# Splitting each load of weights into its high and low part in one step or in two

## The chip, the cores and the metric

The kernel runs on one core of a Trainium2 chip. The core has a matrix engine (TensorE, PE in the profile; its weight loads stand as PEld), a vector engine (DVE), a scalar engine (ACT), GpSimd (POOL) and a queue processor (SP) that issues most of the DMAs. Every engine works through its own instructions in the order in which the program lists them, and waits on semaphores for the others. The metric is the device time of one execution in microseconds. Before the change it was 1292.62 us, the median of three runs (1292.37 to 1294.42).

## The reference

One layer of an encoder over 1024 tokens of width 1024, in float32:

```
h = rmsnorm(x, norm1_w);  z = h @ w_in                      # 1024 x 2852
A: 8 heads of sparse attention: an indexer scores keys, the 256 best per query are kept,
   softmax over those with a position bias, times values
B: 8 heads of chunkwise retention with rotary, group norm and a swish gate
x = x + concat(A, B) @ w_out                                # 1024 x 1024
h2 = rmsnorm(x, norm2_w)
x = x + (silu(h2 @ w_gate) * (h2 @ w_up)) @ w_down          # hidden width 2816
```

All of the large products go through weights that are used once: w_in, w_out, w_gate, w_up and w_down.

## The kernel before

To keep float32 accuracy at the speed of the shorter format, each factor is split into a high part, which is the value rounded, and a low part, which is the rest. A product is then three matmuls: high by high, high by low and low by high. For the weights this is done on the chip, chunk by chunk. A chunk is what one pass of TensorE over 512 tokens needs: 256 columns by 1024 rows for the projections and for gate and up, or 512 columns by 512 rows for the down projection. The first chunk of each half of the input projection is 292 columns wide.

The function `pieces` (lines 277 to 311) prepares a chunk. Its generator `fill` goes over the chunk's loads. A load is a DMA of 1024 columns into a tile `wraw`, of which there are three in rotation (line 292); a chunk of 256 or 512 columns has two loads, the last chunks of the down projection one, a chunk of 292 columns four loads of 584 columns. The load is cut into `SUB` = 2 parts. For each part ACT copies and rounds it into `whi` (line 306; the very first load of the program goes through DVE instead, line 304), and DVE subtracts that from `wraw` into `wlo`. The subtraction of a part is held back in `late` until the next part, or the next load, has its turn. The tiles `whi` and `wlo` exist twice, so while TensorE works on one chunk the next one can be prepared.

The order of all instructions is fixed when the program is built. The code walks through the matmuls of the projections; after every three of them `tick` (line 937) asks the threads in `THREADS` (weights "w", selection "sel", attention "att", and so on) whether their next step may be placed there. A step runs a generator up to its next `yield`. It may be placed when the time at which the thread's last step ends, by the planner's own estimates, lies 0.7 us back, and when the estimated work that waits on DVE and on ACT is at most 4.0 us. The estimates are made in `charge` (line 865): an ACT copy of n columns is put at 0.06 + n/1200 us, a DVE subtraction at 0.07 + n/960 us. When a chunk is needed, `weights` (line 982) places whatever is left of its steps at once, and opens the next chunk. So the parts of the weights stand in the queues of ACT and DVE between the small steps of selection, attention and retention.

The second half of the feed-forward block takes gate and up through another path, `chunk_parts` (line 356), in which a load of 1024 columns is split in one step already; it does not go through `pieces`. The down projection there does.

Of the kernel before, what the change touches and what calls it, by code (L numbers as in the profile page):

```python
# [25 lines left out]
C_Q, C_C, C_QB, C_KB, C_VB, C_GB = 0, 512, 804, 1316, 1828, 2340  # L26
NEG = -1.0e30
BIG = 3.0e38
SUB = 2
WARM = 11  # L30
VALUES, PAIRS, GATES = 4, 4, 2

# [86 lines left out]
class Layer:  # L119
# [157 lines left out]
    def pieces(self, loads, step, n, rows):  # L277

        nc = self.nc
        first, self.warm = not self.warm, True  # L280
        hi, lo = self.wpair()
        hi = hi[:, :rows * n].rearrange("p (k n) -> p k n", n=n)
        lo = lo[:, :rows * n].rearrange("p (k n) -> p k n", n=n)

        def fill():
            late = None
            for i, parts in enumerate(loads):
                if late:
                    late()
                    late = None  # L290
                tag, bufs = ("sc", 2) if first and i == 3 else ("wraw", 3)
                raw = (self.at_ if tag == "sc" else self.sb)([128, 1024], tag=tag, bufs=bufs)[:, :step * n].rearrange("p (k n) -> p k n", n=n)
                o = 0
                for src, w in parts:
                    nc.sync.dma_start(raw[:, :, o:o + w], src.rearrange("(k p) n -> p k n", p=128))
                    o += w
                ks = slice(i * step, i * step + step)
                sub = step // SUB if step % SUB == 0 else step
                for k0 in range(0, step, sub):
                    ks = slice(i * step + k0, i * step + k0 + sub)  # L300
                    if late:
                        late()
                    if first and i == 0:
                        nc.vector.tensor_copy(hi[:, ks, :], raw[:, k0:k0 + sub, :])
                    else:
                        nc.scalar.activation(hi[:, ks, :], raw[:, k0:k0 + sub, :], AF.Copy)
                    late = lambda ks=ks, raw=raw, k0=k0: nc.vector.tensor_tensor(
                        lo[:, ks, :], raw[:, k0:k0 + sub, :], hi[:, ks, :].bitcast(F32), op=OP.subtract)
                    yield
            late()  # L310
        return (hi, lo), fill()

    def order(self, j0, g):
# [1087 lines left out]
```

## Time and profile before

| | |
|---|---|
| median of three runs | 1292.62 us |
| the profiled execution | 1296.16 us |
| span of its instructions | 1294.4 us |
| PE busy | 1259.0 us, 97% |
| DVE busy | 999.0 us, 77% |
| ACT busy | 788.7 us, 61% |
| POOL busy | 57.3 us, 4% |

The profiled execution is 3.5 us above the median, and 1.8 us of it lie outside the span. A busy time is the time in which at least one of the engine's instructions is on record; the records of neighbouring instructions overlap, so a busy share near 1 is not an engine at its peak. All instructions stand under one line of the code, L99, because a helper issues them; the tiles' names tell them apart. `d` is the PSUM tile of the projections, `t` and `l` are those of attention and retention.

### The profile page before, as it was taken

The numbers are of one execution on the slowest core, as the hardware profiler recorded it, in microseconds if no ns is written. First come the engines' busy times: TensorE is split into PE (matmuls) and PEld (weight loads), VectorE is DVE, ScalarE is ACT, GpSimd is POOL, SyncE is SP. The second block draws the span as 40 slices with busy tenths as digits, with TensorE's granted clock in tenths as the row PEclk, the third lists the DMA queues.
The fourth block names the chain that finished last, engine by engine and source line by source line (L and its number), as shares of the span: only waits on it lengthen the run. The fifth ranks groups of instructions, "written<-read, shape, count | busy, mean of one in ns | idle before, by whom it ended". The sixth has DMA issues, their size and how long they took to land.

```text
span 1294.4 us, 22648 instructions
## 1 busy us (share of the span) xinstructions
PE 1259.0 (97%) x8363; PEld 1133.8 (88%) x8363; DVE 999.0 (77%) x2592; ACT 788.7 (61%) x1764; POOL 57.3 (4%) x68
## 2 busy tenths in 40 slices
PE   8799998999999999999999999999999999999998
PEld 7799898999999888888888878888988999898987
DVE  6679899888978887878787695645488787776866
ACT  7778977655695778468658944433375454453533
POOL 1401011010120000000000000000000000000000
PEclk8899999999999999999999999999999999999999
DMA  8433213221232132322223222225434242433311
GB/s 270 159 83 85 73 45 105 76 64 52 66 122 91 53 95 68 96 66 73 90 66 96 67 82 81 66 75 203 130 98 147 66 131 72 124 87 110 98 49 66
DMA packets 157791, 121.33 MB, mean 94 GB/s; under 512 B 8176, under 2 KB 137840, under 8 KB 157552
## 3 DMA queue, kind: packets, MB, share of 16 engines
q1 hardware_dynamic: 151744, 111.14, 28.7%
q10 hardware_dynamic: 5936, 8.74, 2.0%
q8 instruction: 65, 1.06, 0.3%
q14 instruction: 46, 0.38, 0.1%
HBM read 115.67 MB, written 4.19 MB: 93 GB/s over the span
## 4 chain that ended last, share of the span: by engine, by line
PE 75%; DVE 11%; ACT 7%; issue 3%; DMA 2%; POOL 1%; SPq 0%; ACTq 0%; POOLq 0%; DVEq 0%
PE d L99 64%; PE t L99 9%; DVE wlo L99 3%; ACT junk L99 3%; PE l L99 2%; DVE L L99 1%; ACT whi L99 1%; ACT Thi L99 1%; ACT waste L99 1%; DMA bias<-in_near_dram 1%; DVE plo L99 1%; DMA wraw<-in_w_down_dram 0%; POOL rc L99 0%; DVE Tlo L99 0%; DVE junk L99 0%
## 5 line engine op out<-in xcount | busy, mean ns | idle before, releaser
L99 PE MATMUL d<-whi,Thi 128*128 128x256 f32 (+2 forms) x1136 | 352.0, 310 | 6.2 <-ACT Thi L99 4.3
L99 PE MATMUL d<-wlo,Thi 128*128 128x256 f32 (+2 forms) x1136 | 342.1, 301 | 1.6 <-DVE wlo L99 1.5
L99 PE MATMUL d<-whi,Tlo 128*128 128x256 f32 (+2 forms) x1136 | 341.7, 302 | 0.0
L99 PEld LDWEIGHTS d<-whi,Thi 128*128 128x128 f32 x1136 | 216.2, 190 | 20.0 <-ACT Thi L99 6.7
L99 PEld LDWEIGHTS d<-wlo,Thi 128*128 128x128 f32 x1136 | 216.4, 191 | 10.1 <-DVE wlo L99 2.3
L99 PEld LDWEIGHTS d<-whi,Tlo 128*128 128x128 f32 x1136 | 216.8, 191 | 8.7 <-DVE Tlo L99 1.1
L99 ACT ACTIVATE whi<-wraw 128x512 fp32r<-128x512 f32 (+1 forms) x300 | 171.7, 616 | 69.0 <-PE d L99 52.6
L99 DVE TENSOR_TENSOR wlo<-wraw,whi 128x512 fp32r<-128x512 f32 (+1 forms) x302 | 197.2, 674 | 6.6 <-ACT whi L99 5.8
L99 ACT ACTIVATE junk<-sc,tc 128x384 bf16<-128x384 f32 (+5 forms) x186 | 163.6, 879 | 33.8 <-DVE tc L99 30.1
L99 PE MATMUL d<-Phi,whi 128*128 128x256 f32 x616 | 172.4, 280 | 1.7 <-ACT u L99 1.0
L99 PE MATMUL d<-Phi,wlo 128*128 128x256 f32 x616 | 171.9, 280 | 1.6 <-DVE wlo L99 1.6
L99 PE MATMUL d<-Plo,whi 128*128 128x256 f32 x616 | 171.6, 279 | 0.0
L99 PE MATMUL d<-Thi,whi 128*128 128x512 f32 (+1 forms) x368 | 143.1, 389 | 0.0
L99 PE MATMUL d<-Tlo,whi 128*128 128x512 f32 (+1 forms) x368 | 141.2, 384 | 0.2 <-DVE Tlo L99 0.2
L99 PE MATMUL d<-Thi,wlo 128*128 128x512 f32 (+1 forms) x368 | 141.2, 384 | 0.0
L99 PEld LDWEIGHTS d<-Phi,whi 128*128 128x128 f32 x616 | 116.6, 189 | 3.1 <-ACT u L99 1.8
L99 PEld LDWEIGHTS d<-Phi,wlo 128*128 128x128 f32 x616 | 116.3, 189 | 2.0 <-DVE wlo L99 1.9
L99 PEld LDWEIGHTS d<-Plo,whi 128*128 128x128 f32 x616 | 116.3, 189 | 0.4
L99 DVE TENSOR_TENSOR x<-d,x 128x512 f32<-128x512 f32 (+1 forms) x64 | 39.1, 623 | 64.2 <-PE d L99 56.5
L99 ACT ACTIVATE whi<-S 128x1024 fp32r<-128x1024 f32 x44 | 45.4, 1056 | 69.4 <-PE d L99 57.0
L99 PEld LDWEIGHTS d<-Thi,wlo 128*128 128x128 f32 x368 | 69.1, 188 | 14.9
L99 PEld LDWEIGHTS d<-Tlo,whi 128*128 128x128 f32 x368 | 69.2, 188 | 12.1 <-DVE Tlo L99 0.5
(334 smaller groups left out, 2349.7 us busy)
## 6 DMA issues: line engine op xcount, KB each, us to landing
wraw<-in_w_down_dram SPq DMA_DIRECT2D x44, 512.0 KB, 3.7
wraw<-in_w_in_dram SPq DMA_DIRECT2D x24, 512.0 KB, 3.8
wraw<-in_w_gate_dram SPq DMA_DIRECT2D x44, 256.0 KB, 3.1
wraw<-in_w_up_dram SPq DMA_DIRECT2D x44, 256.0 KB, 3.5
quad<-in_w_gate_dram SPq DMA_DIRECT2D x44, 256.0 KB, 3.6
quad<-in_w_up_dram SPq DMA_DIRECT2D x44, 256.0 KB, 4.3
wraw<-in_w_in_dram SPq DMA_DIRECT2D x32, 256.0 KB, 3.4
wraw<-in_w_out_dram SPq DMA_DIRECT2D x16, 512.0 KB, 3.8
```

The costliest lines, as they stand in the source:

```text
L99: return f(*args, **kw)
```

## The change

`SUB` becomes 1, so that each load is split by one ACT copy and one DVE subtraction over all of its columns. The first chunk of the program keeps its two parts.

```diff
@@ -26,7 +26,7 @@
-SUB = 2
+SUB = 1
@@ -295,7 +295,7 @@
                 ks = slice(i * step, i * step + step)
-                sub = step // SUB if step % SUB == 0 else step
+                sub = step // (2 if first else SUB)
                 for k0 in range(0, step, sub):
                     ks = slice(i * step + k0, i * step + k0 + sub)
```

A chunk of two loads then has three steps in place of five, one of one load two in place of three, and the 292 column chunk of the second half five in place of nine.

## Rows read from the trace of the kernel before

**Rows 1.** The page: busy time, share and instructions of the engines
```profile
PE 1259.0 (97%) x8363; PEld 1133.8 (88%) x8363; DVE 999.0 (77%) x2592; ACT 788.7 (61%) x1764; POOL 57.3 (4%) x68
```

**Rows 2.** Waits of PE alone: us in total, times, longest us
```profile
PE t L99 <- ACT ct L99: 4.6, 2, 4.3
...
PE d L99 <- DVE wlo L99: 3.1, 3, 1.6
...
PE d L99 <- ACT whi L99: 1.7, 3, 1.1
...
PE d L99 <- DVE Tlo L99: 0.2, 1, 0.2
```

**Rows 3.** Busy time by stage: PE, PEld, DVE, ACT, POOL, clock, DMA share, GB/s
```profile
20.00:425.00 405.00, 389.33 (x3161) 374.20 (x3160) 339.88 (x1257) 289.38 (x828) 51.75 (x55) 0.99 0.31 90
425.00:884.00 459.00, 455.21 (x2314) 378.63 (x2313) 343.31 (x901) 298.99 (x598) 2.59 (x4) 1.00 0.25 76
```

**Rows 4.** Waits of all engines, the longest of ACT, columns as in rows 2
```profile
ACT whi L99 <- PE d L99: 156.0, 53, 9.2
```

**Rows 5.** Groups by form: shapes, count, busy us, mean ns, idle before, releasers
```profile
L99 DVE TENSOR_TENSOR wlo<-wraw,whi 128x512 fp32r<-128x512 f32 x288 | 191.3, 685 | 6.6 <-ACT whi L99 5.8
...
L99 ACT ACTIVATE whi<-wraw 128x512 fp32r<-128x512 f32 x288 | 166.9, 624 | 65.8 <-PE d L99 50.3 <-issue 6.9 <-DVE maA L99 5.2
...
L99 DVE TENSOR_TENSOR wlo<-S,whi 128x1024 fp32r<-128x1024 f32 x44 | 52.9, 1222 | 4.9 <-ACT whi L99 4.8
...
L99 ACT ACTIVATE whi<-S 128x1024 fp32r<-128x1024 f32 x44 | 45.4, 1056 | 69.4 <-PE d L99 57.0 <-DVE S L99 9.2 <-DVE cc L99 3.1
```

**Rows 6.** Timeline of ACT near 980 us: start, us, instruction, count
```profile
978.35 1.06 ACT L99 ACTIVATE whi<-S 128x1024 fp32r<-128x1024 f32 x1 [0.51 <-DVE S L99]
979.31 0.61 ACT L99 ACTIVATE th<-cc 128x512 f32<-128x512 f32 x1
...
984.40 2.18 ACT L99 ACTIVATE whi<-wraw 128x512 fp32r<-128x512 f32 x4
```

**Rows 7.** Timeline of DVE near 980 us
```profile
979.44 1.23 DVE L99 TENSOR_TENSOR wlo<-S,whi 128x1024 fp32r<-128x1024 f32 x1
980.59 0.69 DVE L99 SCALAR_TENSOR_TENSOR th<-th,cc 128x512 f32<-128x512 f32 x1
...
986.40 2.49 DVE L99 TENSOR_TENSOR wlo<-wraw,whi 128x512 fp32r<-128x512 f32 x4
```

**Rows 8.** Timeline of PE: the 292 column chunk of the second half
```profile
199.03 0.40 PE L99 MATMUL d<-whi,Thi 128*128 128x292 f32 x1 [1.06 <-ACT whi L99]
200.04 0.40 PE L99 MATMUL d<-whi,Thi 128*128 128x292 f32 x1 [0.61 <-DVE zqk L99]
```

**Rows 9.** Chain that ended last, in that stretch: start, us, what
```profile
195.44 2.83 DMA mb__3057<-in_xt_dram
...
199.57 0.42 DVE zqk L99
```

**Rows 10.** Groups by form, the waits of 256 column matmuls for low parts
```profile
L99 PE MATMUL d<-wlo,Thi 128*128 128x256 f32 x896 | 251.6, 281 | 0.3 <-DVE wlo L99 0.3
```

**Rows 11.** Timeline of ACT: second chunk, the bias load's issue, the last chunk
```profile
24.12 1.67 ACT L99 ACTIVATE whi<-wraw 128x512 fp32r<-128x512 f32 x3
...
38.09 0.34 ACTq L99 DMA_DIRECT2D bias<-in_near_dram  x1
...
1278.06 0.63 ACT L99 ACTIVATE whi<-wraw 128x512 fp32r<-128x512 f32 x1 [1.09 <-issue]
1278.65 0.63 ACT L99 ACTIVATE Thi<-th 128x512 fp32r<-128x512 f32 x1
```

**Rows 12.** Timeline of DVE: second chunk, the bias
```profile
24.78 1.90 DVE L99 TENSOR_TENSOR wlo<-wraw,whi 128x512 fp32r<-128x512 f32 x3
...
45.54 1.23 DVE L99 TENSOR_TENSOR bias<-bias,far 128x1024 f32<-128x1024 f32 x1 [3.95 <-DMA bias<-in_near_dram]
```

**Rows 13.** Timeline of PE: the second chunk's first matmul
```profile
26.53 0.28 PE L99 MATMUL d<-whi,Thi 128*128 128x256 f32 x1
```

## The prediction

> **What bounds the kernel now.** I read the page first: TensorE is on record as busy for 1259.0 of the 1294.4 us, DVE for 999.0 and ACT for 788.7 [rows 1]. So at most 35.4 us of the span are idle time of the engine that everything feeds, and a change that only shortens work on DVE and ACT can win no more than a part of that. The second view is the list of what TensorE waited for. It has 21 lines, which begin with 4.6 us for a small tile of the key path and end with 0.2 us [rows 2]; all together they are 38 waits and 30.7 us. The parts of the weights, the only thing this change makes, end six of them: 3.1 us for low parts and 1.7 us for high parts [rows 2]. The third view, the busy time by stage, says where there is anything to win or lose. From 20 to 425 us, in the input projection with attention beside it, TensorE idles 405.00 - 389.33 = 15.7 us, and DVE is busy for 84% of the stage; from 425 to 884 us, in the first half of the feed-forward block, it idles 459.00 - 455.21 = 3.8 us [rows 3]. Last, the waits of all engines show who leads: ACT stood before a copy into `whi` for 156.0 us in 53 waits until TensorE had let go of the buffer [rows 4]. The splitting thus works against the buffers, nearly a whole chunk ahead of its use, and not against the clock.
>
> **The change part by part.** The first part is the work itself. By the durations, two copies of 512 columns take 2 x 624 = 1248 ns on ACT and one of 1024 takes 1056; two subtractions on DVE take 2 x 685 = 1370 ns and one 1222 [rows 5]. There are 144 such loads (288 halves), so the durations promise 144 x 0.192 = 27.6 us less on ACT and 144 x 0.148 = 21.3 us less on DVE. That is too much, since neighbouring records overlap. Four copies of 512 in a row took 2.18 us, so each after the first adds (2.18 - 0.62) / 3 = 0.52 us, while the instruction behind a copy of 1024 starts 979.31 - 978.35 = 0.96 us after it [rows 6]. The saving is 2 x 0.52 - 0.96 = 0.08 us a load. On DVE it is 2 x (2.49 - 0.69) / 3 - (980.59 - 979.44) = 1.20 - 1.15 = 0.05 us [rows 7]. I take these: some 11.5 us of ACT and 7 us of DVE in the whole kernel, 1.5% and 0.7% of their busy time. All of it lies beside TensorE's work. Its worth on the path is 0; if that cover were gone the DVE share of it, 7 us, would show. The DMAs are as many and as large as before and stand in the same order on SP. Only the release of a `wraw` tile moves: from its copy's start it took 0.62 + 2 x 0.60 + 0.69 - 0.60, about 1.9 us, with two halves behind each other, and takes 1.06 + 1.22, about 2.3 us, with one. With three tiles in rotation, and splitting a chunk ahead, 0.4 us of delay to a prefetch is hidden: 0, and 0.4 us for each load where it isn't.
>
> The second part is what TensorE waits for directly. Of the six waits for parts, the 256 column chunks have 0.3 us [rows 10], and the 292 column chunk of the second half has 1.06 us at 199.03 us [rows 8]. The rest belongs to the first chunk and to the path of `chunk_parts`, which don't change. The wait at 199.03 looks like a gain: with five steps in place of nine that chunk would be done before its matmuls begin. But one block of matmuls later TensorE waits again, until 200.04, for a tile that DVE frees (`zqk`) [rows 8], and the chain of that stretch goes from a load of x, 195.44 to 198.27 us, to that DVE instruction and not through the weights [rows 9]. What is saved at 199.03 is therefore waited at 200.04. I put the direct waits at -0.2 us, with ends at -1.4 (both waits gone) and +0.4.
>
> The third part is the lead of the second chunk, the one place where a first part becomes urgent. Its copies start at 24.12 and its matmuls at 26.53 us [rows 11, 13], and its subtractions at 24.78 [rows 12]. With one step the first high part is ready at 24.12 + 1.06 = 25.2, and the low part at about 25.2 + 1.22 = 26.4 us, just in time, where the trace has it a us sooner. I put +0.1 us on it; its ends are 0 and +0.5.
>
> The fourth is the load of the bias table. ACT issues it at 38.09 us [rows 11], DVE stands 3.95 us before it lands and goes on at 45.54 [rows 12], and TensorE's longest wait, 4.3 us [rows 2], comes out of that. Before 38.09 ACT copies, by the program's order, the second and the third chunk, eight halves; as four loads they cost 4 x 0.08 = 0.3 us less, of which ACT's own idle time there takes some. I put -0.2 us, with ends at -0.8 (the durations' price) and 0.
>
> The fifth is the last chunk. At 1278.06 ACT copies a half into `whi`, and at 1278.65 the high part of the hidden values, which the last matmuls wait for [rows 11]. A whole load ahead of it costs 1056 - 624 = 0.43 us more, and no work is left to hide it: +0.4 us. Its ends are -0.6, should the planner put the hidden values first, and +0.5.
>
> The sixth is the order. The planner's own price for a load falls by one fixed term on each engine, 0.06 us on ACT and 0.07 us on DVE, and a chunk has three steps in place of five, each of which had to wait 0.7 us after the last. So the steps of all the other threads shift a little, from the second chunk on. No row shows the new order. The nearest rows are the idle times of the stages, 15.7 us and 3.8 us [rows 3]: I bound the effect at -3 us (a fifth of the first stage's) and at +4 us (worked out under the slower rival), and take -0.5, since fewer steps are left over to be placed all at once when a chunk is called for.
>
> The sum is -0.2 + 0.1 - 0.2 + 0.4 - 0.5 = -0.4 us. The profiled execution, 1296.16 us, would become 1295.8; it lies 3.5 us above the median of the three runs, for no reason that the rows show, so I set the sum against the median: 1292.62 - 0.4 = 1292.2 us. About 0.2%, 2.6 us, is what a measurement of this kernel can tell from no change.
>
> **The rivals.** (a) Faster: the shorter thread pulls the others. It needs that the waits in the first 425 us come from queues that run late, for which DVE's 84% in that stage speaks [rows 3]; against it speaks that the two followed here, at the bias load and at 199 us, end on DMAs and not on a full queue [rows 9, 12]. If it holds, half of the 4.3 us wait at the bias load goes, the wait at 199.03 goes with 0.3 us of the 256 column ones, and the stage loses a tenth of its other idle time: -2.1 - 1.4 - 1.0 = -4.5 us, 1288.1 us.
>
> (b) Slower: a long part stands ahead of what TensorE needs. ACT and DVE take their queues in order. Where a half of 685 ns stood before a small result that TensorE waits for, a whole of 1222 ns may stand now: 0.54 us more on DVE, 0.43 on ACT [rows 5]. The place is the stage from 20 to 425 us, where selection, attention and retention pass small results to TensorE between the parts; the hidden values of the last chunk are the same thing. For it speaks that the cadence saves only 0.05 to 0.08 us where a whole instruction costs half a us of latency. Against it speaks that a half which stood behind the small result now may take the other half with it. It decides from five waits that grow by the full price, 5 x 0.54 = 2.7 us; with eight to ten of them it is +4.3 to +5.4, about 1297.2 us. The Trainium skill, in "Perfetto Trace Analysis", section "Optimizing Scalar/DVE Operations", says that larger operations help where the engine is saturated, and that where ACT and DVE are not saturated but cause bubbles elsewhere, breaking instructions up may let work finish sooner. By that rule this change goes the wrong way, as rival (b) has it; with ACT at 61% and DVE at 77% of the span, the trace fits its second case better than its first.
>
> (c) The change does nothing that reaches TensorE, because every part is ready long before its use. That is the forecast with all terms at 0, 1292.6 us, and belongs to the same case.
>
> **How the numbers follow.** The forecast, with (c), has 0.42: the work saved is hidden, and the known terms nearly cancel. Its own range is what counts as no change, 1290.0 to 1295.2 us. Rival (a) gets 0.34, as there are more parts of the program in which fewer steps help than hurt, and (b) 0.24. The predicted time is that of the forecast, 1292.2 us. For the range I add the bounds of the unknown costs: the lower ends come to -1.4 - 0.8 - 0.6 - 3 = -5.8 us at their worst, the upper ones to +0.4 + 0.5 + 0.5 + 4 = +5.4. Not all fall together, so I cut the lower end to -5 and leave the upper at +5: 1287.5 to 1297.5 us, which leaves out the outer part of each rival, about 2 in 10.
>
> **What would show it.** After the change there should be 144 copies and 144 subtractions of 1024 columns from `wraw`, at about 1.06 and 1.22 us, and ACT's and DVE's busy time lower by 10 to 28 and 7 to 22 us. If the forecast is right, TensorE's idle time stays within 33 to 38 us, with the wait at 199 us replaced by a longer one for `zqk` and the one before the last down projection longer by 0.4 us. Rival (a) would show in the stage from 20 to 425 us as idle time well under 15.7 us, and an earlier issue of the bias load; (b) as more or longer waits there, each with a part of 1024 columns just ahead in the queue of ACT or DVE. The prediction is wrong if the new order makes a stall of several us of a kind that is not in the trace of before, or takes the one at the bias load away.

## The result, and the profile after

The changed kernel takes 1304.52 us (median; 1302.60 to 1305.85), the kernel before beside it 1294.45 us (1292.37 to 1296.37). The ratio is 1.0087, with a 95% interval of 1.0077 to 1.0097: 10.1 us slower, where 1292.2 us was forecast, with 1287.5 to 1297.5 as the range. The profiled execution took 1305.85 us, with a span of 1303.7 us.

The page of the kernel after, busy time and instructions by engine, beside [rows 1]:

```profile
PE 1263.3 (97%) x8363; PEld 1136.5 (87%) x8363; DVE 993.9 (76%) x2444; ACT 776.8 (60%) x1616; POOL 54.4 (4%) x68
```

DVE and ACT have 148 instructions and 5.1 and 11.9 us less. TensorE has the same 8363 matmuls, is busy 4.3 us longer and idle for 1303.7 - 1263.3 = 40.4 in place of 35.4 us. The two make up the 9.3 us by which the span grew. The saving was there, and TensorE lost all the same.

Busy time by stage after, columns as in [rows 3] (length, then PE, PEld, DVE, ACT, POOL, granted clock, DMA share, GB/s):

```profile
20.00:425.00 405.00, 385.27 (x3110) 369.63 (x3109) 331.97 (x1191) 280.06 (x767) 49.27 (x55) 0.98 0.31 90
425.00:884.00 459.00, 452.63 (x2298) 376.92 (x2298) 340.17 (x837) 291.23 (x527) 2.21 (x4) 1.00 0.26 76
```

Between 20 and 425 us TensorE idles 19.7 us instead of 15.7, at a clock of 0.98 instead of 0.99, and has started 51 matmuls fewer at the end of it; at the stage's mean of 385.27 / 3110 = 0.12 us each that is, as an estimate, 6 of the 9.3 us. From 425 to 884 us it idles 6.4 us instead of 3.8. The loss lies where selection and attention run beside the matmuls.

The first stage is a gain and a loss. Cut at 220 us, before

```profile
20.00:220.00 200.00, 187.04 (x1495) 179.11 (x1494) 166.97 (x659) 157.19 (x477) 31.49 (x35) 0.97 0.36 105
220.00:425.00 205.00, 202.29 (x1669) 195.09 (x1668) 172.91 (x599) 132.19 (x351) 20.27 (x20) 1.00 0.26 76
```

and after:

```profile
20.00:220.00 200.00, 191.15 (x1548) 183.27 (x1547) 165.47 (x628) 155.57 (x456) 29.36 (x36) 0.99 0.38 109
220.00:425.00 205.00, 194.12 (x1564) 186.36 (x1564) 166.50 (x564) 124.50 (x312) 19.90 (x19) 0.98 0.24 71
```

TensorE's idle time falls from 13.0 to 8.9 us before 220 us and rises from 2.7 to 10.9 us behind it.

What TensorE waits for after (us in total, times, longest), beside [rows 2]:

```profile
PE t L99 <- DVE kn L99: 5.4, 5, 3.4
PE t L99 <- DVE L L99: 4.1, 2, 2.8
PE d L99 <- ACT Thi L99: 4.0, 3, 1.6
PE t L99 <- DVE te L99: 3.9, 1, 3.9
...
PE d L99 <- DVE wlo L99: 2.8, 2, 1.6
...
PE d L99 <- ACT whi L99: 1.0, 2, 0.7
```

The parts of the weights, the only thing the change makes, are waited for less than before: 2.8 us for low parts instead of 3.1, 1.0 us for high parts instead of 1.7. What has grown is the wait for `te`, the end of the top-k of one token block, and one of 2.8 us for `L`, the scaled queries of an attention. Before, no wait for `te` was longer than 1.1 us:

```profile
PE t L99 <- DVE te L99: 1.8, 2, 1.1
```

The longest one of `kn`, 3.4 us, is the old wait at the bias load under another name (below).

The stall at `te` in full; it stands before the fifth attention. First TensorE after, from its timeline (start, length, instruction, idle time before it):

```profile
418.93 0.28 PE L99 MATMUL d<-wlo,Thi 128*128 128x256 f32 x1
419.04 0.28 PE L99 MATMUL d<-whi,Tlo 128*128 128x256 f32 x1
423.27 1.09 PE L99 MATMUL t<-eye,L 128*128 128x128 f32 x4 [3.94 <-DVE te L99]
424.01 0.56 PE L99 MATMUL d<-whi,Thi 128*128 128x256 f32 x1
```

Then DVE after in the same stretch:

```profile
415.57 1.23 DVE L99 TENSOR_TENSOR wlo<-wraw,whi 128x1024 fp32r<-128x1024 f32 x1 [0.60 <-ACT whi L99]
...
418.62 1.22 DVE L99 TENSOR_TENSOR wlo<-wraw,whi 128x1024 fp32r<-128x1024 f32 x1
...
420.59 1.49 DVE L99 TENSOR_TENSOR_SCAN L<-junk 128x640 f32<-128x640 bf16 x1
...
422.44 0.69 DVE L99 TENSOR_TENSOR L<-q,rq 128x512 f32<-128x512 f32 x1
```

And the same two places in the kernel before, on DVE

```profile
409.42 0.67 DVE L99 TENSOR_TENSOR L<-q,rq 128x512 f32<-128x512 f32 x1
```

and on TensorE:

```profile
413.55 0.60 PE L99 MATMUL t<-eye,L 128*128 128x128 f32 x4
```

Before, the scaled queries were ready at 409.42 + 0.67 = 410.1 us and TensorE took them at 413.55: 3.5 us to spare. After, they are ready at 423.13 us, 13.0 us later, and TensorE is there at about 419.16 (one step of 0.12 behind 419.04), 5.6 us later. 13.0 - 5.6 = 7.4 us of slip against 3.5 us to spare leaves 3.9 us, which is the wait. (The profile puts it down to `te`, which DVE finished last before 423.27; the matmul reads the queries, `L`.) Two whole subtractions of 1.2 us each stand in the end of that chain, but they don't explain 7.4 us: the first round of this top-k already starts 17.8 us later on ACT, before

```profile
340.81 0.83 ACT L99 ACTIVATE junk<-sc,tc 128x640 bf16<-128x640 f32 x1
```

and after:

```profile
358.61 0.83 ACT L99 ACTIVATE junk<-sc,tc 128x640 bf16<-128x640 f32 x1 [1.33 <-DVE tc L99]
```

Behind the stall TensorE also runs slower. Windows of the kernel after, columns as above:

```profile
419.00:423.30 4.30, 0.35 (x4) 0.18 (x2) 4.19 (x9) 0.00 (x0) 0.00 (x0) 0.93 0.22 65
423.30:424.80 1.50, 1.50 (x8) 1.50 (x9) 1.46 (x2) 0.41 (x1) 0.00 (x0) 0.50 0.00 0
424.80:426.30 1.50, 1.50 (x9) 1.50 (x9) 1.47 (x4) 1.37 (x3) 0.00 (x0) 0.56 0.02 5
426.30:428.00 1.70, 1.70 (x17) 1.70 (x17) 1.64 (x3) 0.18 (x1) 0.00 (x0) 1.00 0.00 0
```

The granted clock is 0.50, which is 1.2 GHz, then 0.56, then 1.00, which is 2.4 GHz. That is 0.50 x 1.5 + 0.44 x 1.5 = 1.4 us on top: the one stall costs 5.3 us.

A second stall of this kind, at the queries of the third attention, costs more. TensorE after, and two windows behind it:

```profile
225.49 1.11 PE L99 MATMUL t<-eye,L 128*128 128x128 f32 x4 [2.84 <-DVE L L99]
```

```profile
225.49:228.50 3.01, 3.01 (x14) 3.01 (x15) 3.01 (x6) 1.73 (x3) 0.00 (x0) 0.50 0.03 3
228.50:231.50 3.00, 3.00 (x16) 3.00 (x15) 2.92 (x5) 0.93 (x4) 0.00 (x0) 0.50 0.87 230
```

Before, at the same queries, on DVE and on TensorE:

```profile
218.95 0.68 DVE L99 TENSOR_TENSOR L<-q,rq 128x512 f32<-128x512 f32 x1
```

```profile
219.69 0.66 PE L99 MATMUL t<-eye,L 128*128 128x128 f32 x4
```

Before, the queries were ready at 219.63 us and TensorE came at 219.69: nothing to spare, and no wait. After, TensorE waits 2.84 us and then runs for 6.0 us at 0.50, which is 3.0 us on top, 5.8 us in all. The two stalls together come to some 11 us.

### The profile page after: what moved, and what is told of

It reads as the page before. It is cut to its first block, busy times and chain, and to the rows that moved or that the text cites. A ratio compares the mean times of both kernels' runs of the same rounds, so it can differ in the third digit from the quotient of the medians.

```text
span 1303.7 us, 22328 instructions
## 1 busy us (share of the span) xinstructions
PE 1263.3 (97%) x8363; PEld 1136.5 (87%) x8363; DVE 993.9 (76%) x2444; ACT 776.8 (60%) x1616; POOL 54.4 (4%) x68
## 3 DMA queue, kind: packets, MB, share of 16 engines
q8 instruction: 65, 1.06, 0.3%
## 4 chain that ended last, share of the span: by engine, by line
PE 71%; DVE 12%; ACT 7%; issue 4%; DMA 3%; POOL 1%; SPq 0%; POOLq 0%; ACTq 0%; DVEq 0%
PE d L99 59%; PE t L99 10%; DVE wlo L99 4%; ACT junk L99 3%; PE l L99 2%; ACT whi L99 1%; DMA quad<-in_w_gate_dram 1%; DVE L L99 1%; DVE Tlo L99 1%; DVE S L99 1%; DMA bias<-in_near_dram 1%; DVE wraw L99 1%; DVE th L99 1%; DVE cc L99 1%; DMA wraw<-in_w_in_dram 0%
## 5 line engine op out<-in xcount | busy, mean ns | idle before, releaser
L99 DVE TENSOR_TENSOR wlo<-wraw,whi 128x1024 fp32r<-128x1024 f32 (+2 forms) x154 | 180.1, 1179 | 16.0 <-ACT whi L99 15.1
L99 ACT ACTIVATE whi<-wraw 128x1024 fp32r<-128x1024 f32 (+2 forms) x152 | 153.4, 1028 | 63.9 <-PE d L99 49.6
```

The costliest lines, as they stand in the source:

```text
L99: return f(*args, **kw)
```

## The experiments

Two words have to be kept apart, and the description of the kernel above does not: the *sequence*, in which the kernel's own planner issues the instructions, and the *queues* as they are built. The build sorts each engine's instructions once more. In the built program of before at least 425 of the 1500 ACT instructions that the planner places, 910 of the 2468 on DVE and 204 of the 8171 on TensorE would have to be moved to get back to the sequence.

The *place* of an attention is the number of projection matmuls (those into `d`) ahead of its reciprocal `rec` in the sequence. The eight places of before are 563, 989, 1580, 2051, 2735, 3149, 3605, 3989; those of the changed kernel 587, 1001, 1703, 2051, 2747, 3164, 3635, 4091. In the traces 1524 and 1646 such matmul records lie ahead of the third `rec`. One row each from the views of that tile (shortest, median and longest in ns, first and last start), before

```profile
L99 DVE RECIPROCAL rec<-sums x8: 192/201/203, 104.1 to 843.3; 128x8 f32<-128x8 f32 x8
```

and after:

```profile
L99 DVE RECIPROCAL rec<-sums x8: 194/200/204, 104.8 to 877.4; 128x8 f32<-128x8 f32 x8
```

The first attention ends at nearly the same time, the last one 34 us later.

All times, against runs of the kernel before beside them; "third, last" are the places of the third and the last attention:

| kernel | third, last | us | ratio (95%) |
|---|---|---|---|
| changed kernel | 1703, 4091 | +10.1 | 1.0087 (1.0077 to 1.0097) |
| 1 whole, queues held as before, early | 1580, 3989 | +22.1 | 1.0172 (1.0155 to 1.0188) |
| 2 whole, queues held as before, late | 1580, 3989 | +13.6 | 1.0109 (1.0092 to 1.0126) |
| 3 halves, queues held as changed | 1703, 4091 | +12.6 | 1.0094 (1.0079 to 1.0109) |
| 4 before, ACT price 0.061 | 1616, 3989 | +1.5 | 1.0013 (1.0004 to 1.0023) |
| 5 whole on ACT alone | 1577, 3989 | +9.0 | 1.0066 (1.0045 to 1.0088) |
| 6 whole on DVE alone | 1541, 4016 | +1.1 | 1.0008 (0.9998 to 1.0017) |
| 7 whole in the input projection | 1703, 3989 | +5.3 | 1.0044 (1.0029 to 1.0059) |
| 8 whole in the first half behind it | 1580, 4076 | +2.3 | 1.0019 (1.0009 to 1.0028) |
| 9 whole, sequence of before | 1580, 3989 | +0.1 | 1.0006 (0.9997 to 1.0015) |
| 10 halves, sequence of changed | 1703, 4091 | +4.6 | 1.0039 (1.0027 to 1.0052) |
| 11 changed, ACT price 0.061 | 1628, 4076 | +2.1 | 1.0022 (1.0012 to 1.0033) |
| 12 quarters | 1505, 3905 | +7.8 | 1.0063 (1.0051 to 1.0075) |
| 13 halves, selection held back | 1697, 4091 | +7.0 | 1.0056 (1.0044 to 1.0069) |
| 14 whole, selection brought forward | 1517, 4052 | +3.4 | 1.0029 (1.0019 to 1.0038) |
| 15 changed, DVE price 0.071 | 1706, 4091 | +9.6 | 1.0075 (1.0063 to 1.0088) |
| 16 halves, selection a little earlier | 1523, 3941 | -0.9 | 0.9993 (0.9984 to 1.0001) |
| 17 whole on ACT, sequence of before | 1580, 3989 | -0.1 | 1.0003 (0.9994 to 1.0012) |
| 18 whole, selection and attention forward | 1526, 3932 | +2.5 | 1.0019 (1.0009 to 1.0028) |

**Order or length, with the queues held (1 to 3).** An order-only dependency from each instruction to the one before it on its engine holds every queue in a given order; it adds no instruction. Runs 1 and 2 put whole instructions into the queues of before, at the place of the first or of the second half. Run 3 puts two halves behind each other into the queues of the changed kernel.

```
  if k0 == 0:                    # run 2: if k0 + sub == step
      act.activation(hi[:, whole, :], raw, AF.Copy)
...
  for ins in self.made_ins[k]:
      if before is not None:
          self.tc.add_manual_dep(ins, before.name, ...NoSync...)
      before = ins
```

> The loads are split in one step, as in the changed kernel, but every engine gets its instructions in exactly the order of the kernel before: the whole copy stands where the first half's copy stood, the whole subtraction where the first half's subtraction stood, and the second half's places are empty. Theory A (the order is the cause: the long instructions themselves cost nothing): 1291 to 1296 us, within 0.2% of the kernel before, and TensorE's idle time within 2 us of its 35.4. Theory B (rival: a whole part of 1222 ns in the queue ahead of small results is the cause, whatever the order): at least half of the 10 us shows here, 1299 to 1305 us. A mixture lies between 1296 and 1299.

> The same with the whole copy and the whole subtraction where the second half's stood, so that each part is finished later by up to a step. Theory A: again 1291 to 1297 us; if the lead of the weights over their use were the matter it would be slower than the variant with the early places by 2 us or more, which neither theory wants. Theory B: 1299 to 1306 us.

> The other corner: the loads are split in halves, as in the kernel before, but every engine gets its instructions in exactly the order of the changed kernel, two halves back to back where a whole stands there. Theory A (order): 1301 to 1306 us, the changed kernel's time, since only the order differs from the kernel before. Theory B (long instructions): 1292 to 1297 us, because no instruction is longer than before.

Run 1 took 1315.62 us, run 2 1307.14, run 3 1306.19. If only the order were wrong, 1 and 2 would have been as fast as before; if only the length of an instruction were, 3 would have been. All three are slower, by 12.6 to 22.1 us, but the holding itself, on an unchanged kernel, was not timed, so these runs refute neither theory. In run 2 one wait that before does not have shows what rival (b) meant, a matmul that stands for a low part (waits of TensorE in run 2; the line is that of the enforced issue):

```profile
PE d L99 <- DVE wlo L319: 2.3, 1, 2.3
```

That is 2.3 of run 2's 13.6 us. A held queue is not what the build makes, either. From here on the queues are free.

**A small change of the order (4).**

```
- cost = 0.06 + 0.08 * hasattr(kw.get("scale"), "shape") + ...
+ cost = 0.061 + 0.08 * hasattr(kw.get("scale"), "shape") + ...
```

> The kernel before with the planner's estimate of an ACT instruction raised from 0.060 to 0.061 us plus columns. No instruction changes, only the order in which the planner lays them out. Theory A in its strong form (any small shift of the planner's estimates gives another order, and orders differ by some us): the time moves by more than 0.2%, to either side, and may come near the changed kernel's 1304. If it is the fewer steps of this change in particular that hurt, the time stays at 1293 to 1296 us. Theory B: 1293 to 1296 us.

1295.05 us, +1.5, with the same instructions. That is short of the 0.2% that the strong form of theory A wanted, and within the 1293 to 1296 us of the other readings: this shift of the sequence of before does not lose 10 us.

**Which engine (5, 6).** Whole copies with half subtractions, and half copies with whole subtractions, each with the sequence that the planner then makes.

```
# run 5
nc.scalar.activation(hi[:, ks, :], raw, AF.Copy)
yield
for ks, r in halves: ...one subtraction a half
# run 6
for part, r in halves:
    nc.scalar.activation(hi[:, part, :], raw[:, r, :], AF.Copy)
late = lambda ...: nc.vector.tensor_tensor(lo[:, ks, :], raw, hi[:, ks, :]..., op=OP.subtract)
```

> The copy on ACT is one instruction for a load of 1024 columns (the first chunk apart), the two subtractions on DVE stay halves, each in a step of its own. Theory G (granularity: a whole load's work, put down as one block, stands ahead of small results that TensorE waits for): the loss of 10 us of the changed kernel splits by engine; DVE is the fuller one (busy 999 of 1294 us against 789 for ACT) and its whole costs 0.54 us more than a half against 0.43 us on ACT, so ACT alone gives a third of it or so: +2 to +5 us, 1296 to 1299 us. Rival O (it is only that any other order is worse by chance): a new order is drawn here too, and the time falls anywhere between +0 and +12 us, with no relation to the engine. Rival N (the steps count, not the columns: fewer yields bunch the thread): the number of steps here is about as before, so +0 to +2 us.

> The two copies on ACT stay halves but are issued one behind the other in one step, the subtraction on DVE is one instruction for a load of 1024 columns (the first chunk apart). Theory G: both engines now have a block as long as a whole load (two adjacent halves block ACT for 1.1 us, as a whole does), so the whole loss is there again: +8 to +14 us, 1302 to 1308 us. If only DVE mattered, the same; if only ACT's length of one instruction mattered, +0 to +3 us. Rival O: anywhere between +0 and +12 us, with no relation to the run that has wholes on ACT alone.

Run 5 took 1301.92 us, its four executions 1297.23 to 1303.10; run 6 took 1294.04. That went against the granularity theory as it was put down: the fuller engine, DVE, can have its wholes, in the sequence that comes with them, for 1.1 us. It left run 5, with the attentions where they were, as a riddle (run 17).

**Which stretch (7, 8).** Whole loads in the 22 chunks of the input projection alone (but for its first), and alone in the next 38, output projection and feed-forward block of the first half.

```
  self.nth = getattr(self, "nth", -1) + 1
  parts_of = 1 if 0 <= self.nth < 22 and not first else SUB    # run 8: 22 <= self.nth < 60
...
  sub = step // parts_of
```

> Whole loads only in the chunks of the input projection (to about 425 us of the kernel before), halves in all others. In the changed kernel the pauses of TensorE between 20 and 216 us shrank by 5 us and those from 216 to 425 us grew by 10 us. Theory G with the place that the traces show: +4 to +7 us here, 1298 to 1301 us, with the stall of 4 us at the start of the out projection. Rival O: anywhere from -3 to +10 us. Rival T (the loss comes from the tail and the feed-forward block): +0 to +1 us.

> Whole loads only in the output projection, gate, up and down chunks of the first half (from about 385 to 884 us of the kernel before), halves in all others. In the changed kernel the pauses of TensorE from 425 to 648 us grew by 4 us, those from 648 to 884 us by nothing. Theory G: only the stretch in which attention blocks still run beside it pays, +2 to +5 us, 1296 to 1299 us; together with the run that has wholes in the input projection alone it makes up the 10 us. Rival O: the two do not add up to 10 us. Rival T: +3 to +9 us, all of it here.

1298.22 and 1295.28 us: 5.3 and 2.3 us, both inside what was expected, but together 7.6 us and not the 10 that theory G wanted from the two. The 16 chunks that are left, of the second half, were not tried alone. The longest wait of TensorE in run 7 is the stall of the changed kernel again, with halves behind it:

```profile
PE t L99 <- DVE te L99: 5.7, 1, 5.7
```

**The sequence and the instructions, taken apart (9, 10).** In run 9 the planner still counts and places halves, as before; the instruction issued at the first half's place is a whole. In run 10 the planner counts a whole, as in the changed kernel, and two halves are issued there.

```
# run 9
self.charge("scalar", "activation", (hi[:, ks, :], raw[:, k0:k0 + sub, :], AF.Copy), {})
if k0 == 0:
    act.activation(hi[:, whole, :], raw, AF.Copy)
# run 10
self.charge("scalar", "activation", (hi[:, ks, :], raw, AF.Copy), {})
for dst, src in both:
    act.activation(hi[:, dst, :], raw[:, src, :], AF.Copy)
```

> Whole copies and subtractions at the place where the first half stood, in the sequence that the planner laid out for the kernel before (it still counts two halves); only the build's own sorting of each engine's queue, which sees the longer instructions, is free. In that sequence the third block's attention ends after 1580 matmuls of the projections, as in the kernel before; in the changed kernel it ends after 1703. Theory P (the planner places selection and attention later when a load is one step): with the old sequence the loss is gone, +0 to +3 us, 1293 to 1296 us. Theory G (a whole load's work is one block ahead of small results, wherever it stands): the loss stays, +8 to +14 us, 1301 to 1307 us.

> Halves everywhere, two behind each other at the place of a whole, in the sequence that the planner laid out for the changed kernel (it still counts one whole); the build's own sorting of the queues sees halves and may put a small instruction between them. The third block's attention ends after 1703 matmuls, as in the changed kernel. Theory P: the loss is there without a single whole instruction, +8 to +12 us, 1301 to 1305 us. Theory G: since a small result may now go between the halves, +1 to +5 us, 1294 to 1298 us.

Run 9 took 1294.17 us beside 1294.06: no difference. Its page shows the changed kernel's instructions (148 fewer on both engines than in [rows 1])

```profile
PE 1258.3 (97%) x8363; PEld 1131.3 (87%) x8363; DVE 990.3 (77%) x2444; ACT 774.9 (60%) x1616; POOL 57.2 (4%) x68
```

and its attentions end where they did before:

```profile
L99 DVE RECIPROCAL rec<-sums x8: 191/198/204, 101.0 to 842.2; 128x8 f32<-128x8 f32 x8
```

In this sequence the whole instructions cost nothing. Run 10, without a single one of them, took 1298.62 us, half of the loss, and has the stall:

```profile
PE t L99 <- DVE te L99: 4.7, 1, 4.7
```

At +4.6 us it misses the +8 to +12 of theory P and lies in the +1 to +5 of theory G, so the sequence does not do all of it by itself: in this sequence the wholes cost some 5 us more than two halves each, in the sequence of before nothing.

**Another sequence for the same instructions (11, 15).** The changed kernel, with one price of the planner raised by 0.001 us: ACT's in run 11, DVE's in run 15.

```
- cost = 0.07 + 0.06 * scalars + n / (1920.0 if quick else 960.0)
+ cost = 0.071 + 0.06 * scalars + n / (1920.0 if quick else 960.0)    # run 15
```

> The changed kernel with the planner's fixed price of an instruction on ACT at 0.061 in place of 0.060 us; no instruction is other than in the changed kernel, only the sequence. In it the third block's attention ends after 1628 matmuls in place of 1703, the last one's after 4076 in place of 4091. Theory P: the part of the loss that comes from the third block goes, 3 to 6 us of the 10, so 1297 to 1301 us. Theory G: the blocks are the same, so 1302 to 1306 us, as the changed kernel.

> The changed kernel with the planner's fixed price of an instruction on DVE at 0.071 in place of 0.070 us; only the sequence differs. The third block's attention ends after 1706 matmuls and the last after 4091, as late as in the changed kernel (1703, 4091). Theory P: the loss stays, +7 to +12 us, 1301 to 1306 us. Rival O: a new draw, anything from 0 to +12 us.

Run 11 brings the third attention from 1703 to 1628 and takes 1296.18 us, 2.1 us over before, less than was expected; from 400 to 432 us TensorE has no wait of more than 0.8 us, and none for `te`. Run 15 leaves it at 1706 and takes 1303.07 us, +9.6. Its waits of TensorE from 400 to 432 us:

```profile
PE t L99 <- DVE te L99: 5.0, 1, 5.0
```

These are the same instructions three times, and 10.1, 2.1 and 9.6 us.

**The suspected cause alone, and taken out (13, 14, 16, 18).** The planner lets a thread take its next step some time after its last; that time is changed for the selection thread, in run 18 for attention too. Halves in 13 and 16, the changed kernel in 14 and 18.

```
- "sel": (4.0, 1, 0.7)
+ "sel": (4.0, 1, 1.5)      # run 13; run 14: 0.5; run 16: 0.65
+ "sel": (4.0, 1, 0.4), ... "att": (4.0, 1, 0.4)      # run 18
```

> The kernel before, halves everywhere, but the planner lets the selection thread take its next step 1.5 us after its last in place of 0.7. The third block's attention then ends after 1697 matmuls of the projections (1580 before, 1703 in the changed kernel), the fifth's after 2771 (2735, 2747), the last after 4091 (3989, 4091). Theory P (the late place of the selection carries the loss): +6 to +12 us, 1300 to 1306 us, with a stall of TensorE of 3 to 5 us near 420 us in front of the transposes of the scaled queries. Rival O (any sequence but the one of before has its own stalls, the selection's place says nothing): anything from 0 to +12 us, without that stall.

> The changed kernel, but the planner lets the selection thread take its next step 0.5 us after its last in place of 0.7. The third block's attention ends after 1517 matmuls (1580 before, 1703 in the changed kernel), the fifth's after 2702, the last after 4052. Theory P: the two stalls near 225 and 423 us go, 7 us of the 10, so 1294 to 1298 us. Rival O: anything from 0 to +12 us.

> The kernel before, halves everywhere, but the planner lets the selection thread take its next step 0.65 us after its last in place of 0.7. The third block's attention ends after 1523 matmuls in place of 1580, the last after 3941 in place of 3989. Theory P in its plain form: a little faster, 0 to -3 us, 1291 to 1294 us. Rival O: 0 to +12 us. Between them: once the selection no longer ends late, its place decides nothing, within 2 us of before.

> The changed kernel, but the planner lets the selection and the attention thread take their next step 0.4 us after their last in place of 0.7. The attentions end after 551, 935, 1526, 1964, 2693, 3083, 3539 and 3932 matmuls, all earlier than in the kernel before. Theory P in its plain form: no stall from a late selection is left, -1 to +2 us, 1292.5 to 1295.5 us. Rival O (any sequence but the one of before has stalls of its own): +2 to +8 us, as the runs with whole copies alone (+8.5) and with quarters (+7.8), whose attentions were no later than before either.

Run 13, the kernel before planned with a late selection, takes 1300.47 us: +7.0, inside the 6 to 12 expected. The stall that was expected near 420 us is not there, though, as rival O had it; from 400 to 432 us TensorE waits for other tiles

```profile
PE t L99 <- DVE wraw L99: 2.3, 1, 2.3
PE d L99 <- DVE te L99: 0.4, 1, 0.4
```

and the last attention ends later still than in the changed kernel:

```profile
L99 DVE RECIPROCAL rec<-sums x8: 193/200/205, 97.2 to 889.2; 128x8 f32<-128x8 f32 x8
```

Run 14 takes 1296.86 us: with the selection brought forward the changed kernel loses 3.4 us in place of 10.1, and TensorE's longest wait is 0.9 us from 216 to 235 us and 0.5 us from 400 to 432 us, so both stalls are gone. Run 18 takes 1295.74 us, +2.5, just above what the plain form of the theory allows (+2) and inside rival O's +2 to +8. Run 16 takes 1292.58 us, -0.9 with an interval that reaches 1.0001: earlier than in time is worth nothing that can be told from zero. So a sequence with a late selection is enough to lose most of what was lost, and one with an earlier selection gives most of it back, but not all. Each of these runs has a whole sequence of its own, and run 13 loses its time at other waits than the changed kernel; that lateness as such is the cause is not shown.

**Finer still (12).**

```
- sub = step // SUB if step % SUB == 0 else step
+ sub = step // 2 if first else max(1, step // 4)
```

> Every load of the 256 column chunks is split in four steps of one row block each in place of two; the others and the first chunk as before. It adds some 0.08 us on ACT and 0.05 us on DVE for each added pair, 200 instructions on each engine. The planner ends the attentions earlier: the third after 1505 matmuls of the projections in place of 1580, the last after 3905 in place of 3989. Theory P: the time follows that place, so a gain of 1 to 5 us if anything, 1288 to 1293 us. Theory G: a finer grain helps too, 1 to 4 us, less the added work. Rival S (the step size is at its best at halves because the added work of quarters meets a DVE that is 84% busy in the first 425 us): +2 to +6 us, 1295 to 1299 us.

1301.85 us, +7.8, although every attention is earlier than before. Theory P said a gain or nothing; this is a miss, and above rival S too. The waits differ again, with these two among the longest of TensorE, and no one cause was isolated for them:

```profile
PE d L99 <- DVE maA L99: 2.4, 1, 2.4
...
PE d L99 <- ACT ci L99: 2.0, 1, 2.0
```

**The riddle of run 5 (17).** Whole copies, half subtractions, in the sequence of before.

```
  if k0 == 0:
      act.activation(hi[:, whole, :], raw, AF.Copy)
...
  dve.tensor_tensor(lo[:, ks, :], raw[:, k0:k0 + sub, :], hi[:, ks, :]..., op=OP.subtract)
```

> Whole copies on ACT at the place of the first half, half subtractions on DVE, all in the sequence that the planner laid out for the kernel before (attentions after 563, 989, 1580, 2051, 2735, 3149, 3605, 3989 matmuls). Theory P, in the wider form that the sequence carries all of the loss: -1 to +2 us, 1292.5 to 1295.5 us. Rival A (a whole copy on ACT before half subtractions on DVE costs something of its own): +5 to +9 us, 1298 to 1303 us, as in the run with its own sequence.

1293.16 us beside 1293.21. The 9.0 us of run 5 belong to its sequence as well, one whose selection is not late.

**What stands.** Shown: the whole instructions are free in the sequence of before (9, 17); the loss comes with the sequence that the planner makes for them (11 and 15 against the changed kernel, 10 without wholes); the same halves, planned with a late selection, lose 7.0 us (13). All five kernels with free queues whose third attention ends at 1697 or later lose 4.6 to 10.1 us; of the other eleven, nine lie between -0.9 and +3.4 us, and two lose 9.0 and 7.8 (5, 12). The place of the third attention is thus a sign of a slow sequence, and not more: the fourth's, 2051, is the same before and after, and the stall at 423 us stands at the fifth, whose place moves by 12. Open: what in the sequences of runs 5 and 12 costs that much; why the wholes cost 5 us more than halves in the changed sequence and nothing in the old one; and which decision of the planner moves the selection. Whole loads on one engine alone leave the third attention at 1577 or 1541, on both they move it to 1703, and 0.001 us on a price moves it by 75 matmuls. None of the planner's decisions was tried by itself.

## Why the prediction was wrong, step by step

**The work saved** was sized rightly. There are 144 whole loads, as counted, and 4 of 584 columns besides (by form: count, busy us, mean ns, idle before; beside [rows 5]):

```profile
L99 DVE TENSOR_TENSOR wlo<-wraw,whi 128x1024 fp32r<-128x1024 f32 x144 | 174.7, 1221 | 16.0 <-ACT whi L99 15.1
...
L99 ACT ACTIVATE whi<-wraw 128x1024 fp32r<-128x1024 f32 x144 | 149.1, 1054 | 62.0 <-PE d L99 49.6 <-issue 8.0 <-DVE mb__5833 L99 1.9
```

The forecast from the cadence, 11.5 us on ACT and 7 on DVE, meets 11.9 and 5.1; the durations would have had 27.6 and 21.3. Per merged pair that is 11.9 / 148 = 80 ns and 5.1 / 148 = 34 ns. The Trainium skill, "Perfetto Trace Analysis", section "Optimizing Scalar/DVE Operations", gives some 93 and 60 ns as the fixed cost of such an instruction on SBUF, and says that profiled durations hold about twice that. The durations here gave 192 and 148 ns. Run 9 has the same merged pairs in the sequence of before, where less else changes; there busy time falls by (788.7 - 774.9) / 148 = 93 ns on ACT and (999.0 - 990.3) / 148 = 59 ns on DVE, and the trace agrees with the page. That the saving is worth 0 on the path is what run 9 shows as well. The splitting still leads; ACT waits for TensorE before a copy into `whi` nearly as long as in [rows 4]:

```profile
ACT whi L99 <- PE d L99: 149.8, 49, 9.2
```

**The direct waits**, put at -0.2 us, were -1.0 by the totals for low and high parts, within their ends. At the 292 column chunk (TensorE after, beside [rows 8])

```profile
196.82 0.40 PE L99 MATMUL d<-whi,Thi 128*128 128x292 f32 x1 [0.69 <-ACT whi L99]
197.40 0.41 PE L99 MATMUL d<-whi,Thi 128*128 128x292 f32 x1 [0.17 <-DVE zqk L99]
```

both waits shrank, 1.06 to 0.69 and 0.61 to 0.17 us. The reasoning that the second would take up what the first gave was wrong, on a small term.

**The second chunk** needed nothing: its first whole subtraction starts at 25.04 us, its first matmul at 26.37 without a wait (26.53 before, [rows 13]).

**The bias load** is issued at 35.63 us in place of 38.09 [rows 11], 2.5 us earlier and not 0.3. DVE's wait for it (beside [rows 12])

```profile
44.10 1.23 DVE L99 TENSOR_TENSOR bias<-bias,far 128x1024 f32<-128x1024 f32 x1 [3.19 <-DMA bias<-in_near_dram]
```

falls from 3.95 to 3.19 us, and TensorE's longest wait with it from 4.3 to 3.4 us. At about -0.9 us that is slightly beyond the -0.8 of its lower end. The shorter copies alone, at 0.3 us, are too little for it, and the new sequence alone is no better: ACT issues the load early in run 9, wholes in the sequence of before,

```profile
34.85 0.44 ACTq L99 DMA_DIRECT2D bias<-in_near_dram  x1
```

and late in run 10, halves in the changed sequence:

```profile
37.43 0.33 ACTq L99 DMA_DIRECT2D bias<-in_near_dram  x1
```

So the earlier issue goes with the wholes here, and not with the planner's new sequence; by which step of the build is not shown.

**The last chunk** came as forecast. TensorE near the end, after,

```profile
1288.62 0.50 PE L99 MATMUL d<-whi,Thi 128*128 128x512 f32 x1 [1.60 <-ACT Thi L99]
```

and before:

```profile
1279.34 0.50 PE L99 MATMUL d<-whi,Thi 128*128 128x512 f32 x1 [1.25 <-ACT Thi L99]
```

0.35 us more, where +0.4 was put down.

**The order** is the step that failed. The other five come to 0 - 1.0 + 0 - 0.9 + 0.35, about -1.5 us by what was measured, and the span grew by 9.3, so the sixth must be near +11 us, against a value of -0.5 and ends of -3 and +4. The two stalls at 225 and 423 us, with the slower clock behind them, are about as much; the balance is not closed by that, since TensorE also idles 4.1 us less before 220 us and 2.6 us more from 425 to 884 us. Some 5 of these 11 us show only with whole instructions in this sequence (10), and why is open. Its upper end was five to ten waits that each grow by half a us, taken from the price of one instruction standing in another's way. What moved was a thread. The top-k has 31 rounds, each from ACT to DVE and back, and when these rounds start 17.8 us later (358.61 against 340.81), what counts is how much time the tile at the end of it had to spare. Rows of the trace before could have told: the queries of 409.42 us were ready 3.5 us ahead of TensorE, those of 218.95 us 0.06 us. The step went no further than the idle time of a stage, which says what is lost already, and not how near the rest is to being lost.

**Rival (b)** had the right sign, at 0.24, and half of the size: +4.6 us from parts of 1024 columns ahead of small results. They do stand there, at 415.57 and 418.62 us. But in the sequence of before the same wholes cost nothing (9, 17), so their length by itself is not the cause; the 5 us that they add in the changed sequence (10) may be this rival's mechanism, which no run shows or rules out. The rule of the Trainium skill that stood beside it, that breaking up instructions may let work finish sooner where ACT and DVE are not saturated but make another engine wait ("Perfetto Trace Analysis", "Optimizing Scalar/DVE Operations"), speaks for quarters over halves; run 12 is 7.8 us slower, in a sequence of its own, and wholes are as fast as halves in run 9. In this kernel the runs do not bear it out. **Rival (a)** expected idle time well under 15.7 us in the first stage; it is 19.7. The gain that it looked for is there up to 220 us (4.1 us less idle time) and is lost twice over behind it. **Rival (c)** is what run 9 shows with the sequence kept.

What was named as a sign of being wrong, "a stall of several us of a kind that is not in the trace of before", is what came, in size if not in name: a wait for `te` of 1.1 us was there.

## What to carry to other kernels

Where a planner places the work, a change of one instruction's size is two changes, and the second one, the new sequence, can be the larger by far: issue the new instructions in the old sequence (run 9), and both kernels under a price moved by a hair (runs 4 and 11), before believing either. To bound what a new sequence can cost, read for each result that the bound engine takes from a long serial thread how long it lay ready; a thread that slips by more than that stalls the engine for the rest, and here the engine was slow behind both stalls as well. And the scatter among neighbouring sequences, here -1 to +10 us, is the margin against which a gain of a few us must be judged.

## What was not expected of the hardware

After TensorE had stood for 3.94 us at 419 us, its granted clock was 0.50 for 1.5 us and 0.56 for the 1.5 us after that, which added 1.4 us, a third of the stall itself. After it had stood for 2.84 us until 225.49 us, the clock was 0.50 for 6.0 us, which added 3.0 us: the shorter stall cost more in all. In run 10 the wait at the same matmul was 1.98 us, and the clock from 224.70 to 231.00 us was 1.00.

What the clock takes shows as *busy* time: of the 9.3 us that the span grew, 4.3 are TensorE's busy time on the same 8363 matmuls. The slow stretches behind the two stalls come to 4.4 us, but the kernel before has such stretches too (0.50 from 201.2 to 204.5 us, for one): by the mean clock of the whole span, 0.992 before and 0.991 after, only about 1.4 us of the growth are the clock's, and what makes up the rest is open. Idle time alone would have shown half of the loss.
